# The low parts of sixteen input tiles and eight gate tiles: their subtraction moves from VectorE to GpSimd

## The chip, the cores and the metric

The kernel runs on one core of a Trainium2 chip. The metric is the device time of one execution in microseconds (us). Engines are named as in the profile: PE is TensorE, DVE is VectorE, ACT is ScalarE, POOL is GpSimd and SP is SyncE. PEld is TensorE's loading of weights, which overlaps its matmuls. Each engine works through its own queue in order, and an instruction that waits for a semaphore holds up all that stands behind it in that queue.

## The reference, cut to what matters

One inference step of two layers over 640 tokens (512 latent, 128 context), width 1024, in fp32. Layer 0 is attention and a feed-forward, layer 1 a gated linear recurrent unit and a feed-forward.

```python
def _swiglu(x, w_gu, w_down):
    gate, up = jnp.split(x @ w_gu, 2, axis=-1)
    return (jax.nn.silu(gate) * up) @ w_down

def _rglru_coeffs(xc, w_a, b_a, w_i, b_i, lam):
    ...
    r = jax.nn.sigmoid(jnp.einsum('btnk,nkj->btnj', xb, w_a).reshape(B, T, D) + b_a)
    i = jax.nn.sigmoid(jnp.einsum('btnk,nkj->btnj', xb, w_i).reshape(B, T, D) + b_i)
    ...

def _lru_mixer(xm, h0, w_in, conv_w, conv_b, w_a, b_a, w_i, b_i, lam, w_out):
    gate, xr = jnp.split(xm @ w_in, 2, axis=-1)
    ...
    return y @ w_out, jnp.stack([hT_f, hT_b], axis=1)
```

The tiles of the change belong to `w_in` (1024 x 2048, the recurrent unit's input weights) and to `w_a` and `w_i` (its gate weights). They are prepared in the first feed-forward and used in the recurrent unit after it.

## The kernel before

**Products in three terms.** TensorE multiplies in fp32r, a shorter form of fp32. To keep precision, every operand is split into a high part (its value cast to fp32r) and a low part (value minus high part, again fp32r). A product is three matmuls in one PSUM bank: high by high (line 245), high by low input (246), low weight by high input (247). Weights are tiles of 128 x (8 x 128), so 128 x 1024; inputs are held transposed, with 640 token columns, which go in two chunks of 320. One weight tile (a "unit") thus has 2 x 8 x 3 = 48 matmuls.

**Splitting a weight.** `unit` loads the raw tile on SyncE's queue, casts it on ScalarE (line 189, `whi` or `whx`), and subtracts on VectorE (line 194, `wlo` or `wlx`). For most weights this is done just ahead of their use. The recurrent unit's input weights (`in_wi`, 16 tiles of 128 x 1024) and gate weights (`in_wg`, 8 tiles of 128 x 512) have their low parts made earlier, during the first feed-forward, and written to DRAM. There SyncE's queue reads them back when the recurrent unit runs: line 191 for `lowi`, line 1433 for `lowg`.

**The first feed-forward** (`ffn`, layer 0) has three groups of 8, 7 and 7 hidden tiles of 128. For each hidden tile, a gate unit and an up unit run. VectorE scales the gate's PSUM (line 1042), ScalarE applies SiLU (1044), VectorE scales the up's PSUM (1050) and multiplies (1053), and the product is split (ScalarE's cast at 1551, VectorE's low part at 1553, tiles `big`). After each group, `project` multiplies by the down weights and VectorE adds each result to the residual `x` (line 673). PSUM banks for chunks are three called `mm` and two called `mx`; a bank is free for a new chunk when VectorE has read it.

**The early low parts** (`lows`, a generator). `request` loads a tile twice on GpSimd's queue: cast to fp32r into `mprod` (one buffer, line 307), and plain into `mraw` (two buffers, line 309). The subtraction of line 316 then writes the low part over `mraw`, and line 319, on GpSimd's queue, stores it to DRAM. Then the next tile is requested. `ahead` hands out these steps: each call adds 2 to an account, a large tile costs 3 and a small one 2; it is called once for every gate or up unit after hidden tile 12, and for every tile of the down-projections of the second and third group. `pin` keeps an instruction behind a named one in the order of the program. That order is otherwise set by a scheduler, which simulates a timeline.

The same two tags, `mprod` and `mraw`, serve the modulation columns before (`mod_cols`: GpSimd's queue loads `mraw` at line 270, VectorE multiplies and sums at line 274). Behind the last low part, GpSimd's next work is line 633, a small step of the norm ahead of the recurrent unit.

Of the kernel before, what the change touches and what calls it, by code (L numbers as in the profile page):

```python
# [9 lines left out]
F32 = mybir.dt.float32  # L10
F32R = mybir.dt.float32r
AF = mybir.ActivationFunctionType
ALU = mybir.AluOpType
# [116 lines left out]
class _Step:  # L130
# [170 lines left out]
    def lows(self):  # L301
        nc = self.nc

        def request(key, src):
            shape = list(src.shape)
            hi = self.t(shape, F32R, "mprod", 1, self.sb)
            nc.gpsimd.dma_start(hi, src)
            raw = self.t(shape, F32R, "mraw", 2, self.sb)
            nc.gpsimd.dma_start(raw.bitcast(F32), src)
            return key, raw, hi  # L310
        held = request(*self.split_ahead[0])
        yield 3
        for n in range(len(self.split_ahead)):
            key, raw, hi = held
            with self.pin(self.done):
                nc.vector.tensor_tensor(raw, raw.bitcast(F32), hi.bitcast(F32), ALU.subtract)  # L316
            shape = list(raw.shape)
            self.low_parts[key] = self.dram.tile(shape, F32, tag=f"low{key[0]}{key[1]}", name=f"low{key[0]}{key[1]}")
            nc.gpsimd.dma_start(self.low_parts[key], raw.bitcast(F32))
            if n + 1 < len(self.split_ahead):  # L320
                held = request(*self.split_ahead[n + 1])
            yield 3 if shape[1] == KT else 2
# [794 lines left out]
    def project_halves(self, w, hi, lo, gk, key, xd, ended, opening):  # L1117
# [23 lines left out]
        both = sides[0] + sides[1]  # L1141
        highs(KT - 3, both)
        lows(KT - 3, both)
        highs(KT - 2, both)
        for f in (3, 4):
# [18 lines left out]
        with self.pin(self.done):  # L1164
            lows(KT - 2, both)
        lows(KT - 1, sides[0])
        added = self.added
        part(3, ((0, hi), (0, lo)))
# [562 lines left out]
```

## Time and profile before

| what | value |
| --- | --- |
| median of 3 runs | 1506.03 us (1503.84 to 1506.76) |
| the profiled execution | 1504.18 us, of which its span is 1502.4 us |
| TensorE busy | 1471.8 us, 98% of the span |
| VectorE busy | 1067.6 us, 71% |
| ScalarE busy | 700.0 us, 47% |
| GpSimd busy | 270.3 us, 18% |
| line 316, 24 times | first start 569.2 us, last 751.9 us |

The span runs from the first to the last instruction of the profiled execution, and times in rows count from its start. A row of a group reads: line, engine, operation, output <- inputs by the program's names, shapes, count | busy us, mean ns of one | idle us of that engine just ahead of the group, and what ended most of it. A row of the timeline reads: start, duration, engine, line, operation, names, shape, and in brackets the engine's idle time ahead of it with its releaser. "issue" as a releaser means that the profile shows nothing that the engine waited for. The granted TensorE clock was 0.999 of full speed over the span.

### The profile page before, as it was taken

The numbers are of one execution on the slowest core, as the hardware profiler recorded it, in microseconds if no ns is written. First come the engines' busy times: TensorE is split into PE (matmuls) and PEld (weight loads), VectorE is DVE, ScalarE is ACT, GpSimd is POOL, SyncE is SP. The second block draws the span as 40 slices with busy tenths as digits, with TensorE's granted clock in tenths as the row PEclk, the third lists the DMA queues.
The fourth block names the chain that finished last, engine by engine and source line by source line (L and its number), as shares of the span: only waits on it lengthen the run. The fifth ranks groups of instructions, "written<-read, shape, count | busy, mean of one in ns | idle before, by whom it ended". The sixth has DMA issues, their size and how long they took to land. (4 is left out here: it accounts for less than half of the span.)

```text
span 1502.4 us, 26467 instructions
## 1 busy us (share of the span) xinstructions
PE 1471.8 (98%) x10463; PEld 1442.7 (96%) x10463; DVE 1067.6 (71%) x2035; ACT 700.0 (47%) x1277; POOL 270.3 (18%) x344
## 2 busy tenths in 40 slices
PE   9999999999999999999999999999999999999997
PEld 7999999899999999989899999999999999999997
DVE  5778998689999997544454669786975665655655
ACT  5676666664332123211232479874634342524243
POOL 0212232101111111212200110000331323232311
PEclk9999999999999999999999999999999999999999
DMA  9645765345666667776631454445243131313221
GB/s 377 200 127 180 194 185 168 99 165 181 196 187 195 209 200 259 263 265 222 203 94 51 131 186 139 138 132 214 96 139 98 57 113 57 113 57 101 69 57 70
DMA packets 83547, 232.45 MB, mean 155 GB/s; under 512 B 9408, under 2 KB 25952, under 8 KB 83296
## 3 DMA queue, kind: packets, MB, share of 16 engines
q1 hardware_dynamic: 57360, 142.31, 29.3%
q0 software_dynamic: 25456, 87.77, 18.5%
q8 instruction: 82, 1.34, 0.4%
q10 hardware_dynamic: 608, 0.69, 0.1%
q14 instruction: 41, 0.34, 0.1%
HBM read 204.12 MB, written 19.41 MB: 149 GB/s over the span
## 5 line engine op out<-in xcount | busy, mean ns | idle before, releaser
L245 PE MATMUL mm<-big,whi 128*128 128x320 f32 (+3 forms) x1193 | 368.1, 310 | 4.2 <-ACT gl L1565 1.5
L246 PE MATMUL mm<-big,whi 128*128 128x320 f32 (+3 forms) x1193 | 370.8, 311 | 0.6 <-DVE big L1553 0.6
L247 PE MATMUL mm<-big,wlo 128*128 128x320 f32 (+3 forms) x1193 | 368.7, 310 | 0.0
L245 PEld LDWEIGHTS mm<-big,whi 128*128 128x128 f32 x1193 | 223.9, 188 | 6.8 <-ACT gl L1565 2.1
L246 PEld LDWEIGHTS mm<-big,whi 128*128 128x128 f32 x1193 | 224.3, 188 | 2.2 <-DVE big L1553 1.1
L247 PEld LDWEIGHTS mm<-big,wlo 128*128 128x128 f32 x1193 | 224.6, 188 | 1.1
L274 DVE SCALAR_TENSOR_TENSOR mprod<-mraw,csb 128x1024 f32<-128x1024 f32 x160 | 195.2, 1220 | 10.2 <-DMA mraw<-in_wm 9.5
L673 DVE SCALAR_TENSOR_TENSOR x<-mm,G,x 128x128 f32<-128x128 f32 (+3 forms) x193 | 77.8, 434 | 63.0 <-PE mm L247 61.6
L245 PE MATMUL mm<-big,whx 128*128 128x320 f32 (+3 forms) x363 | 112.3, 309 | 4.8 <-DVE up L1050 1.9
L189 ACT CAST whi<-raw 128x1024 fp32r<-128x1024 f32 (+1 forms) x70 | 72.8, 1040 | 92.3 <-PE mm L246 61.0
L246 PE MATMUL mm<-big,whx 128*128 128x320 f32 (+3 forms) x363 | 112.4, 310 | 1.9 <-DVE big L1553 1.9
L247 PE MATMUL mm<-big,wlx 128*128 128x320 f32 (+3 forms) x363 | 112.2, 309 | 0.0
L270 POOL DMA_DIRECT2D mraw<-in_wm x80 | 43.4, 543 | 345.1 <-DVE mprod L274 258.8
L194 DVE TENSOR_TENSOR wlo<-raw,whi 128x1024 fp32r<-128x1024 f32 (+1 forms) x71 | 85.6, 1206 | 12.6 <-ACT whi L189 12.5
L245 PE MATMUL mx<-big,whi 128*128 128x320 f32 (+3 forms) x299 | 92.1, 308 | 0.7 <-DVE sg L1042 0.7
L246 PE MATMUL mx<-big,whi 128*128 128x320 f32 (+3 forms) x299 | 92.1, 308 | 0.0
L247 PE MATMUL mx<-big,wlo 128*128 128x320 f32 (+3 forms) x299 | 91.8, 307 | 0.0
L316 DVE TENSOR_TENSOR mraw<-mraw,mprod 128x1024 fp32r<-128x1024 f32 (+1 forms) x24 | 25.1, 1048 | 80.4 <-DMA mprod<-in_wi 43.0
L189 ACT CAST whx<-raw 128x1024 fp32r<-128x1024 f32 (+1 forms) x38 | 38.9, 1023 | 81.8 <-PE mm L246 48.5
L245 PE MATMUL mx<-big,whx 128*128 128x320 f32 (+3 forms) x234 | 72.5, 310 | 2.1 <-DVE up L1050 2.1
L245 PEld LDWEIGHTS mm<-big,whx 128*128 128x128 f32 x363 | 68.4, 188 | 5.6 <-DVE up L1050 2.2
L1551 ACT CAST whi<-raw 128x1024 fp32r<-128x1024 f32 (+1 forms) x41 | 41.3, 1007 | 68.3 <-PE mm L246 43.6
(421 smaller groups left out, 3878.4 us busy)
## 6 DMA issues: line engine op xcount, KB each, us to landing
raw<-in_gu SPq DMA_DIRECT2D x88, 512.0 KB, 3.7
mraw<-in_wm POOLq DMA_DIRECT2D x80, 512.0 KB, 3.9
raw<-in_dn SPq DMA_DIRECT2D x24, 512.0 KB, 3.6
sw<-in_wm SPq DMA_DIRECT2D x16, 512.0 KB, 10.2
raw<-in_wqk SPq DMA_DIRECT2D x16, 512.0 KB, 5.0
mraw<-in_wi POOLq DMA_DIRECT2D x16, 512.0 KB, 5.0
mprod<-in_wi POOLq DMA_DIRECT2D x16, 512.0 KB, 5.9
lowi<-mraw POOLq DMA_DIRECT2D x16, 512.0 KB, 2.9
```

The lines of the kernel that those rows point to most:

```text
L189: nc.scalar.copy(hi, raw)
L194: self.low = nc.vector.tensor_tensor(lo, raw, hi.bitcast(F32), ALU.subtract).ins
L245: nc.tensor.matmul(ps, hi[:, k], xhi[:, k, s], start=(k == 0), stop=False)
L246: nc.tensor.matmul(ps, hi[:, k], xlo[:, k, s], start=False, stop=False)
L247: self.done = nc.tensor.matmul(ps, lo[:, k], xhi[:, k, s], start=False, stop=(k == last)).ins
L270: nc.gpsimd.dma_start(w, self.i["wm"][l * 6 + j - 2, f])
L274: nc.vector.scalar_tensor_tensor(prod, w, 1.0, self.csb[:, s], ALU.mult, ALU.mult, accum_out=out[:, s, f:f + 1])
L316: nc.vector.tensor_tensor(raw, raw.bitcast(F32), hi.bitcast(F32), ALU.subtract)
L673: self.added = self.nc.vector.scalar_tensor_tensor(xs, ps[:, a - t0:b - t0], G[:, s, f:f + 1], xs, ALU.mult, ALU.add).ins
L1551: self.nc.scalar.copy(hi, v)
```

## The change

In `lows`, the subtraction is issued on GpSimd instead of VectorE; its operands, its pin, and the loads and the store around it are as they were.

```diff
         for n in range(len(self.split_ahead)):
             key, raw, hi = held
             with self.pin(self.done):
-                nc.vector.tensor_tensor(raw, raw.bitcast(F32), hi.bitcast(F32), ALU.subtract)
+                nc.gpsimd.tensor_tensor(raw, raw.bitcast(F32), hi.bitcast(F32), ALU.subtract)
             shape = list(raw.shape)
             self.low_parts[key] = self.dram.tile(shape, F32, tag=f"low{key[0]}{key[1]}", name=f"low{key[0]}{key[1]}")
             nc.gpsimd.dma_start(self.low_parts[key], raw.bitcast(F32))
```

The scheduler's order changes with it on three engines; ScalarE's and SyncE's queues read the same as before.

VectorE, from the end of the second down-projection (`x` is the residual, fed by PSUM banks `mm` and `mx`) into the third group's gate and up units (`sg`, `up`). `mraw` and `mprod` are the tile to be split and its high part:

```order
 L673 SCALAR_TENSOR_TENSOR x_4130<-mx_7992,G_680_3223,x_4130 128x320
-L316 TENSOR_TENSOR mraw_8760<-mraw_8760,mprod_8758 128x1024
 L673 SCALAR_TENSOR_TENSOR x_4130<-mm_8015,G_680_3223,x_4130 128x192
 L673 SCALAR_TENSOR_TENSOR x_4130<-mm_8015,G_680_3223,x_4130 128x128
 L194 TENSOR_TENSOR wlo_8409<-raw_8406,whi_8408 128x1024
 L1042 TENSOR_TENSOR sg_8081<-mm_8054,r_4705 128x320
-L316 TENSOR_TENSOR mraw_8831<-mraw_8831,mprod_8829 128x512
 L1042 TENSOR_TENSOR sg_8081<-mx_8085,r_4705 128x320
 L194 TENSOR_TENSOR wlx_8478<-raw_8475,whx_8477 128x1024
-L316 TENSOR_TENSOR mraw_8971<-mraw_8971,mprod_8969 128x512
 L1050 TENSOR_TENSOR up_8152<-mm_8125,r_4705 128x320
```

Three subtractions leave this part of VectorE's queue, and what stands around them keeps its order.

GpSimd's queue at the same place:

```order
 L309 DMA mraw_8831<-in_wg 128x512
+L316 TENSOR_TENSOR mraw_8760<-mraw_8760,mprod_8758 128x1024
 L319 DMA lowi_8827<-mraw_8760 128x1024
 L307 DMA mprod_8829<-in_wg 128x512
 L309 DMA mraw_8971<-in_wg 128x512
+L316 TENSOR_TENSOR mraw_8831<-mraw_8831,mprod_8829 128x512
 L319 DMA lowg_8967<-mraw_8831 128x512
 L307 DMA mprod_8969<-in_wg 128x512
```

Each subtraction stands just ahead of the store of its own result, behind the plain load of the next tile; the DMA issues keep their order.

TensorE, at the start of the second down-projection, where two `mm` banks are filled from the last hidden tile's high part (`big_6420`) and low part (`big_6421`):

```order
 L245 MATMUL mm_7609<-big_6420,whx_7582 128x320
 L246 MATMUL mm_7609<-big_6421,whx_7582 128x320
+L246 MATMUL mm_7586<-big_6421,whx_7582 128x320
+L247 MATMUL mm_7586<-big_6420,wlx_7583 128x320
 L247 MATMUL mm_7609<-big_6420,wlx_7583 128x320
 L245 MATMUL mx_7646<-big_6420,whi_7642 128x320
```

The two matmuls that close bank `mm_7586` stood nine rows further down before. Nothing else moves on TensorE.

## The prediction

> **What bounds the kernel now.** I read the page's totals first, then busy time by stretch, the lines of TensorE inside the stretch, the line that is moved, and the timelines of VectorE, TensorE and GpSimd around one stall.
>
> ```profile
> span 1502.4 us, 26467 instructions
> PE 1471.8 (98%) x10463; PEld 1442.7 (96%) x10463; DVE 1067.6 (71%) x2035; ACT 700.0 (47%) x1277; POOL 270.3 (18%) x344
> ```
>
> TensorE is the bound: 98% of the span. A change that takes work from VectorE is worth only what TensorE now waits for it. The stretch is found by busy time (columns: length; TensorE, its weight loads, VectorE, ScalarE, GpSimd; granted clock; DMA).
>
> ```profile
> 569.00:590.00 21.00, 21.00 (x145) 21.00 (x144) 16.32 (x28) 6.12 (x12) 3.76 (x7) 1.00 0.64 229
> 590.00:755.00 165.00, 153.51 (x1033) 151.49 (x1032) 80.05 (x129) 34.96 (x66) 35.52 (x66) 1.00 0.71 240
> 755.00:820.00 65.00, 65.00 (x431) 65.00 (x430) 32.93 (x60) 21.29 (x44) 0.00 (x0) 1.00 0.25 73
> ```
>
> The 24 moved subtractions run from 569 to 752 us. In the first row TensorE never stops; in the second it lacks 165.00 - 153.51 = 11.5 us; in the third, the same feed-forward without the subtractions, it lacks nothing. All 11.5 us end on VectorE, or on ScalarE behind it (idle time and releaser stand last, for 560 to 770 us):
>
> ```profile
> L246 PE MATMUL mm<-big,whx 128*128 128x320 f32 (+1 forms) x137 | 42.6, 311 | 1.9 <-DVE big L1553 1.9
> L245 PE MATMUL mm<-big,whx 128*128 128x320 f32 (+1 forms) x137 | 42.6, 311 | 4.8 <-DVE up L1050 1.9 <-ACT big L1551 1.7 <-DVE x L673 1.2
> L245 PE MATMUL mm<-big,whi 128*128 128x320 f32 (+1 forms) x131 | 40.6, 310 | 1.9 <-DVE up L1050 1.5 <-DVE x L673 0.4
> L245 PE MATMUL mx<-big,whi 128*128 128x320 f32 (+1 forms) x92 | 28.5, 310 | 0.7 <-DVE sg L1042 0.7
> L245 PE MATMUL mx<-big,whx 128*128 128x320 f32 (+1 forms) x85 | 26.3, 310 | 2.1 <-DVE up L1050 2.1
> ```
>
> VectorE is busy for only 80 of these 165 us, so it is not short of time. It stands still in front of the line that is moved:
>
> ```profile
> L316 DVE TENSOR_TENSOR mraw<-mraw,mprod 128x1024 fp32r<-128x1024 f32 (+1 forms) x24 | 25.1, 1048 | 80.4 <-DMA mprod<-in_wi 43.0 <-DMA mprod<-in_wg 24.0 <-issue 13.4
> ```
>
> 25.1 us of work and 80.4 us of standing, mostly for the load of the high part: 105.5 us in which nothing behind it in VectorE's queue can run. How that reaches TensorE (VectorE first, then TensorE's idle times):
>
> ```profile
> 692.85 1.22 DVE L316 TENSOR_TENSOR mraw<-mraw,mprod 128x1024 fp32r<-128x1024 f32 x1 [4.86 <-DMA mprod<-in_wi]
> 694.00 0.67 DVE L673 SCALAR_TENSOR_TENSOR x<-mm,G,x 128x192 f32<-128x192 f32 x2
> 694.58 1.22 DVE L194 TENSOR_TENSOR wlx<-raw,whx 128x1024 fp32r<-128x1024 f32 x1
> 695.71 0.55 DVE L673 SCALAR_TENSOR_TENSOR x<-mx,G,x 128x320 f32<-128x320 f32 x1
> 701.38 1.23 DVE L316 TENSOR_TENSOR mraw<-mraw,mprod 128x1024 fp32r<-128x1024 f32 x1 [5.12 <-DMA mprod<-in_wi]
> 710.23 0.69 DVE L316 TENSOR_TENSOR mraw<-mraw,mprod 128x512 fp32r<-128x512 f32 x1 [5.50 <-DMA mprod<-in_wg]
> ```
>
> ```profile
> 694.81 0.39 PE L245 MATMUL mm<-big,whi 128*128 128x322 f32 x1 [0.41 <-DVE x L673]
> 703.34 0.39 PE L245 MATMUL mm<-big,whx 128*128 128x322 f32 x1 [1.22 <-DVE x L673]
> 711.38 0.41 PE L245 MATMUL mx<-big,whi 128*128 128x322 f32 x1 [0.73 <-DVE sg L1042]
> ```
>
> Between two subtractions VectorE finds about 2.5 us of work (0.67, 1.22, 0.55), then waits 5 us for the next load. It empties PSUM at the pace of that load, one turn in 8.5 us, and TensorE stalls for a free bank about a microsecond after each of these three subtractions starts. The eight stalls of the stretch all follow one of the 24 in this way.
>
> **The change part by part.** Removed from VectorE: 24 subtractions and the waits before them, 105.5 us. What that frees on the path is the 11.5 us. If nothing takes their place, the profiled 1504.18 us (a span of 1502.4 and 1.8 around it, 1.85 below the median of the runs) become 1492.7.
>
> Added to GpSimd: the same 24. No row shows GpSimd writing fp32r, so the price is bounded by its two-input operations on fp32 (shortest, median, longest ns):
>
> ```profile
> L1219 POOL TENSOR_TENSOR sum<-raw,raw x19: 1289/1302/2013, 1084.1 to 1434.1; 128x512 f32<-128x512 f32 x19
> L1107 POOL TENSOR_TENSOR x<-x,c x4: 1001/1490/3651, 1077.9 to 1091.4; 128x320 f32<-128x320 f32 x4
> ```
>
> Line 1219 has one of the two sizes, 128x512: 1.3 us, and by doubling 2.6 us for 128x1024. Line 1107 scaled from 320 to 1024 columns gives 4.8 us by its median and 11.7 by its longest. I take 2.6 and 1.3, from the row of the same width.
>
> The loop on GpSimd's queue: subtract, store (L319), load the next high part (L307), wait for it, subtract.
>
> ```profile
> 694.37 0.54 POOL L319 DMA_DIRECT2D lowi<-mraw  x1 [4.56 <-DVE mraw L316]
> 694.90 0.54 POOL L307 DMA_DIRECT2D mprod<-in_wi  x1
> 589.49 1.23 DVE L316 TENSOR_TENSOR mraw<-mraw,mprod 128x1024 fp32r<-128x1024 f32 x1 [2.39 <-DMA mprod<-in_wi]
> 751.94 0.69 DVE L316 TENSOR_TENSOR mraw<-mraw,mprod 128x512 fp32r<-128x512 f32 x1 [3.56 <-DMA mprod<-in_wg]
> ```
>
> From the subtraction's start (692.85) to its store is 1.52 us; it becomes 2.6, so a turn lengthens by 1.1. The 15 turns from 589.49 to 710.23 took 8.05 us each and would take 9.13; the seven from 710.23 to 751.94 took 5.96 each and, 0.3 longer, would take 6.26. The last subtraction starts near 589.5 + 137 + 44 = 770 and ends at 772. Behind it on GpSimd's queue stands the norm's line 633, which nobody wants before:
>
> ```profile
> 835.39 0.87 POOL L633 TENSOR_TENSOR rs<-var,mhalf 128x3 f32<-128x3 f32 x1 [81.91 <-DVE var L631]
> 836.48 0.32 SPq L191 DMA_DIRECT2D wlo<-lowi  x1
> ```
>
> With TensorE 11.5 us earlier that is 824, so 52 us are left, and the first read of a low part (SyncE, second row) comes after it. GpSimd's longer loop is covered. That cover is gone when a 128x1024 subtraction takes over 2.6 + 52/19 = 5.3 us (15 large ones and eight halves count as 19).
>
> VectorE's first wait after the change is for the modulation weights, which GpSimd now requests 1.1 us later, behind the longer first subtraction:
>
> ```profile
> 577.38 1.23 DVE L274 SCALAR_TENSOR_TENSOR mprod<-mraw,csb 128x1024 f32<-128x1024 f32 x1 [1.88 <-DMA mraw<-in_wm]
> ```
>
> Cost 0 to 1.1 us; I take 0, since TensorE stood nowhere in that stretch and VectorE has a 1.23 us subtraction and a wait less ahead of it.
>
> Two matmuls move: at the start of the second down-projection, the last two of one chunk now stand nine matmuls earlier, 9 x 153.51/1033 = 1.3 us. They need the low part of the last hidden tile:
>
> ```profile
> 644.77 0.42 PE L246 MATMUL mm<-big,whx 128*128 128x320 f32 x1 [1.91 <-DVE big L1553]
> 643.09 1.23 DVE L316 TENSOR_TENSOR mraw<-mraw,mprod 128x1024 fp32r<-128x1024 f32 x1 [2.23 <-issue]
> ```
>
> The subtraction ahead of that tile held it for 2.23 + 1.23 = 3.46 us. Gone, this pays the 1.91 of the stall and the 1.3, barely. Cost 0 to 1.3; I take 0.2.
>
> Contention. When GpSimd and VectorE both work on SBUF tiles, they take turns (GpSimd, VectorE beside it, the same VectorE operation undisturbed):
>
> ```profile
> 1084.13 1.55 POOL L1219 TENSOR_TENSOR sum<-raw,raw 128x512 f32<-128x512 f32 x1
> 1082.93 1.58 DVE L1553 TENSOR_TENSOR big<-x,big 128x320 fp32r<-128x320 f32 x1
> 1095.02 0.48 DVE L1553 TENSOR_TENSOR big<-g,big 128x320 fp32r<-128x320 f32 x1
> ```
>
> 1.58 us instead of 0.48: VectorE lost 1.1 us to one GpSimd operation of 1.3 us. At worst each of the 24 holds VectorE for its whole length: 16 x 2.6 + 8 x 1.3 = 52 us, half of the 105.5 that go. In proportion TensorE would stall 11.5 x 52/105.5 = 5.7 us; at best 0. What decides is a later stretch in which GpSimd adds beside a VectorE busier than it will be here:
>
> ```profile
> 1100.00:1440.00 340.00, 339.75 (x2316) 338.89 (x2315) 202.62 (x327) 129.09 (x208) 99.99 (x72) 1.00 0.28 86
> ```
>
> 100 us of GpSimd additions, and TensorE lacks 0.25 of 340 us. I take 0.3, and keep 5.7 for the range. [...]
>
> Sum: 11.5 - 0 - 0.2 - 0.3 = 11.0 us. The profiled execution would be 1493.2, the median 1506.03 - 11.0 = 1495.0.
>
> **The rivals.** *Lock.* Every subtraction blocks VectorE for its length, as in the 1.58 us row: 1506.0 - 11.5 + 5.7 = 1500.2. Against it stands the row of 340 us.
>
> *No gain.* Another wait lies right behind each stall (a cast on ScalarE, a weight load), and the 11.5 us return under other names: 1504 to 1506. Against it: 65.00 of 65.00 us busy at 755 to 820, and 21.00 of 21.00 at the start, with the same code around.
>
> *Slower.* GpSimd is slow at fp32r, or loses turns to VectorE, as line 1107 did at its longest. Past 5.3 us per subtraction line 633 runs late and TensorE stands at the closing norm; past 2.6 + (52 + 11.5)/19 = 5.9 us the gain is eaten. At 8.25, midway between 4.8 and 11.7, the loop ends 107 us later, at 879, 55 late: 1506.0 - 11.5 + 55 = 1549.5. For it speaks only the longest of line 1107's four.
>
> **How the numbers follow.** Forecast 0.75, lock 0.11, no gain 0.08, slower 0.06. A measurement of this kernel can tell about 0.2%, 3 us. Forecast and lock are both faster: 0.86; unchanged 0.08; slower 0.06. The range starts at the whole 11.5 us off a median that may lie 2.2 lower (the fastest run, 1503.84): 1492.3. It ends just above the lock's 1500.2, at 1501; outside lie no gain and slower, 0.14. The forecast alone spans 1492.3 to 1498.
>
> **What would show it.** VectorE's idle time before line 316 is gone, and TensorE is busy for over 164 of any 165 us in this stretch. GpSimd shows 16 operations of about 2.6 us and 8 of 1.3, the last ending near 772, and line 633 still waits tens of microseconds for VectorE. Wrong: TensorE idle behind VectorE operations stretched by a microsecond or more (lock), TensorE idle behind other releasers (no gain), line 633 starting right after line 319 (slower).

## The result, and the profile after

The changed kernel takes 1491.15 us (median of 4 runs, 1490.91 to 1492.21); beside it the kernel before takes 1506.39 (4 runs, 1503.84 to 1507.95). The ratio is 0.9902, with a 95% interval of 0.9885 to 0.9919. The forecast of 1495.0 had the direction, the place and the mechanism right and the size too small: the time lies 1.15 us below the range's low end of 1492.3. The profiled execution took 1491.32 us, against 1493.2 forecast for it.

The page's totals after:

```profile
span 1489.6 us, 26442 instructions
PE 1470.3 (99%) x10463; PEld 1443.2 (97%) x10463; DVE 1063.6 (71%) x2011; ACT 702.7 (47%) x1277; POOL 321.8 (22%) x368
```

The 24 instructions went from VectorE (2035 to 2011) to GpSimd (344 to 368), and 12.8 us went from the span. VectorE is hardly less busy (1067.6 to 1063.6 us), though 25.1 us of work left it; its timeline below shows why. Busy time by stretch, with the columns as in the prediction; the last row is for a later comparison:

```profile
569.00:590.00 21.00, 21.00 (x145) 21.00 (x144) 14.80 (x27) 5.93 (x13) 5.97 (x8) 1.00 0.59 201
590.00:755.00 165.00, 165.00 (x1124) 165.00 (x1124) 83.90 (x126) 45.10 (x82) 78.34 (x82) 1.00 0.75 246
755.00:820.00 65.00, 65.00 (x425) 65.00 (x425) 28.65 (x48) 15.83 (x32) 6.85 (x9) 1.00 0.27 86
821.80:860.00 38.20, 37.93 (x281) 37.60 (x280) 26.61 (x71) 20.76 (x45) 6.52 (x16) 1.00 0.61 192
```

TensorE lacked 11.5 of 165 us here before; now it lacks nothing, and it starts 1124 matmuls where it started 1033. These 91 matmuls, at the 165.00/1124 = 0.147 us of the same row, are some 13.4 us: more than the idle time that is gone. The prediction's error is already in this one row.

GpSimd, all of line 316 (shortest, median, longest ns, first and last start):

```profile
L316 POOL TENSOR_TENSOR mraw<-mraw,mprod x24: 1284/2394/3052, 570.4 to 768.4; 128x1024 fp32r<-128x1024 f32 x16, 128x512 fp32r<-128x512 f32 x8
```

GpSimd's timeline, one subtraction in the middle and the last one with what follows:

```profile
691.11 2.39 POOL L316 TENSOR_TENSOR mraw<-mraw,mprod 128x1024 fp32r<-128x1024 f32 x1 [2.91 <-DMA mprod<-in_wi]
...
768.36 1.29 POOL L316 TENSOR_TENSOR mraw<-mraw,mprod 128x512 fp32r<-128x512 f32 x1 [3.46 <-DMA mprod<-in_wg]
769.97 0.58 POOL L319 DMA_DIRECT2D lowg<-mraw  x1 [0.31 <-POOL mraw L316]
822.05 0.88 POOL L633 TENSOR_TENSOR rs<-var,mhalf 128x3 f32<-128x3 f32 x1 [51.51 <-DVE var L631]
```

GpSimd now does the standing (2.91 us for the load of the high part, 3.46 at the end), and nobody wants anything of its queue: line 633 waits 51.51 us for VectorE.

VectorE's timeline in the second down-projection, then beside the subtraction at 691.11:

```profile
677.39 0.68 DVE L673 SCALAR_TENSOR_TENSOR x<-mm,G,x 128x192 f32<-128x192 f32 x2 [2.52 <-PE mm L247]
678.33 1.23 DVE L194 TENSOR_TENSOR wlx<-raw,whx 128x1024 fp32r<-128x1024 f32 x1 [0.26 <-ACT whx L189]
680.47 0.55 DVE L673 SCALAR_TENSOR_TENSOR x<-mx,G,x 128x320 f32<-128x320 f32 x1 [0.91 <-PE mx L247]
691.56 3.02 DVE L194 TENSOR_TENSOR wlx<-raw,whx 128x1024 fp32r<-128x1024 f32 x1 [0.45 <-ACT whx L189]
694.51 0.48 DVE L1050 TENSOR_TENSOR up<-mm,r 128x320 f32<-128x320 f32 x1
```

The releasers have turned round: line 673 waited behind line 316's load before, and now waits for TensorE (2.52 and 0.91 us). The fourth row is what the prediction's rival *Lock* is about: a line 194 that takes 1.23 us alone takes 3.02 beside GpSimd's subtraction. It costs VectorE time, and TensorE none in this stretch (165.00 of 165.00 us busy).

### The profile page after: what moved, and what is told of

Read it like the earlier page. It is cut to its first block, busy times and chain, and to the rows that moved or that the text cites. A ratio compares the mean times of both kernels' runs of the same rounds, so it can differ in the third digit from the quotient of the medians.

```text
span 1489.6 us, 26442 instructions
## 1 busy us (share of the span) xinstructions
PE 1470.3 (99%) x10463; PEld 1443.2 (97%) x10463; DVE 1063.6 (71%) x2011; ACT 702.7 (47%) x1277; POOL 321.8 (22%) x368
## 5 line engine op out<-in xcount | busy, mean ns | idle before, releaser
L194 DVE TENSOR_TENSOR wlo<-raw,whi 128x1024 fp32r<-128x1024 f32 (+1 forms) x71 | 87.8, 1237 | 13.6 <-ACT whi L189 13.6
L1219 POOL TENSOR_TENSOR sum<-raw 128x512 f32<-128x512 f32 x19 | 25.6, 1349 | 223.8 <-DMA raw<-in_gu 146.5
L247 PE MATMUL mx<-big,wlx 128*128 128x320 f32 (+3 forms) x234 | 72.6, 310 | 0.0
```

What stands on the lines that cost most here:

```text
L194: self.low = nc.vector.tensor_tensor(lo, raw, hi.bitcast(F32), ALU.subtract).ins
L247: self.done = nc.tensor.matmul(ps, lo[:, k], xhi[:, k, s], start=False, stop=(k == last)).ins
```

## The experiments

Each theory had the same facts to explain: 25.1 us of work and 80.4 us of standing left VectorE, and TensorE gained some 13 us. The standing theory says that only the wait in VectorE's queue mattered. Its rivals: the 25 us of work mattered; GpSimd's new work still costs something; the cover of 52 us is thinner than it looks.

**Work without the wait.** On the kernel before, VectorE subtracts two resident tiles of the same size, and so waits for no load (the pin moves too, from the last matmul to the last subtraction of line 194):

```diff
-            with self.pin(self.done):
-                nc.vector.tensor_tensor(raw, raw.bitcast(F32), hi.bitcast(F32), ALU.subtract)
+            with self.pin(self.low):
+                m = KT * P if key[0] == "i" else 4 * P; nc.vector.tensor_tensor(self.t([P, KT * P], F32R, "mhigh", 1, self.sb)[:, 0:m], self.csb[:, 0, 0:m], self.csb[:, 1, 0:m], ALU.subtract)
```

> VectorE keeps 24 subtractions of the old sizes at about the old places, but takes them from tiles that lie ready (the conditioning vectors), into a scratch tile; nothing waits for a load there. The loads and stores of the early tiles go on without a subtraction (what is stored are the raw tiles). Theory 'standing': only the wait in front of the subtraction cost anything, the 25 us of work nothing: 1490.5 to 1493 us, TensorE idle under 1 us between 569 us and the norm's line 633. Rival 'work': the work itself held TensorE up, at least in its share of the 105.5 us, 25/105.5 of about 14 us, so 3 us or more: 1494.5 to 1500 us.

Measured: 1491.53 us (1490.99 to 1491.86, 4 runs), ratio 0.9924 (0.9907 to 0.9942). VectorE's group, and the stretch:

```profile
L316 DVE TENSOR_TENSOR mhigh<-csb 128x1024 fp32r<-128x1024 f32 (+1 forms) x24 | 25.0, 1040 | 0.0
```

```profile
590.00:744.00 154.00, 154.00 (x1050) 154.00 (x1049) 83.97 (x134) 41.56 (x75) 35.27 (x65) 1.00 0.80 264
```

All 25.0 us of work are back on VectorE with no idle time ahead of them, and TensorE stands nowhere. The work was worth nothing. It does not lie at quite the old places: the 24 start between 576.4 and 790.4 us, where they had started between 569.2 and 751.9.

**The wait without the work.** On the changed kernel, VectorE first subtracts one column of both loaded tiles into a scratch column, so it waits for the same loads:

```diff
+                col = lambda t: t.rearrange(...)[:, 0:1].bitcast(F32); nc.vector.tensor_tensor(self.t([P, 1], F32, "mhigh", 1, self.sb), col(raw), col(hi), ALU.subtract)
                 nc.gpsimd.tensor_tensor(raw, raw.bitcast(F32), hi.bitcast(F32), ALU.subtract)
```

> The changed kernel, and VectorE in addition reads one column of both loads of each early tile (128x1, 24 times) before GpSimd subtracts. VectorE thus stands for the same loads with next to no work. Theory 'standing': the stalls come back, 1500 to 1507 us, with VectorE idle 60 us or more in front of these 24. Rival 'work': 1491 to 1493 us, as the changed kernel.

Measured: 1500.99 us (1498.30 to 1506.71, 10 runs), ratio 0.9989 (0.9973 to 1.0004). VectorE's group, TensorE's longest stall in the second group's down-projection, and the granted clock around it (the last but two of a row's numbers):

```profile
L316 DVE TENSOR_TENSOR mhigh<-mraw,mprod 128x1 f32<-128x1 f32 x24 | 3.8, 159 | 82.8 <-DMA mprod<-in_wi 54.3 <-DMA mprod<-in_wg 24.1 <-issue 4.4
```

```profile
643.29 0.63 PE L245 MATMUL mm<-big,whx 128*128 128x320 f32 x1 [3.93 <-ACT big L1551]
```

```profile
638.00:643.00 5.00, 1.35 (x10) 1.09 (x8) 3.33 (x5) 0.22 (x1) 2.83 (x2) 0.92 0.43 145
...
647.00:649.00 2.00, 2.00 (x9) 2.00 (x8) 1.22 (x2) 0.00 (x0) 0.00 (x0) 0.50 1.07 383
649.00:651.00 2.00, 2.00 (x15) 2.00 (x15) 0.45 (x2) 0.00 (x0) 1.08 (x1) 1.00 0.98 344
```

3.8 us of work and 82.8 of standing bring nearly the whole time back. The pair of runs settles it: with the work and without the wait the gain is whole; with the wait and almost no work, nothing that can be told from no change is left of it. The last view shows something that no row of before had: behind this stall of 3.93 us TensorE runs at a granted clock of 0.50, 9 matmuls in 2 us instead of 15. More on this below.

**No subtraction at all.** On the changed kernel, the line is left out:

```diff
-                nc.gpsimd.tensor_tensor(raw, raw.bitcast(F32), hi.bitcast(F32), ALU.subtract)
+                pass
```

> The changed kernel without the 24 subtractions on any engine; loads and stores stay (what is stored are the raw tiles). Theory 'free on GpSimd': the same as the changed kernel within 0.5 us, 1490.7 to 1492 us. Rival 'lock': VectorE and TensorE still pay for turns taken with GpSimd, so this one is 1 to 5.7 us faster, 1485.5 to 1490 us.

Measured: 1490.94 us (1490.38 to 1492.38, 4 runs), ratio 0.9921 (0.9906 to 0.9937), so 0.2 us from the changed kernel's median, within both spreads. VectorE's line groups from 569 to 800 us, first of the changed kernel, then of this one:

```profile
L194 DVE TENSOR_TENSOR wlx<-raw,whx 128x1024 fp32r<-128x1024 f32 (+1 forms) x17 | 23.7, 1392 | 4.9 <-ACT whx L189 4.9
L1053 DVE SCALAR_TENSOR_TENSOR sg<-up,bias,sg 128x192 f32<-128x192 f32 (+2 forms) x36 | 18.8, 551 | 0.8
```

```profile
L194 DVE TENSOR_TENSOR wlx<-raw,whx 128x1024 fp32r<-128x1024 f32 (+1 forms) x17 | 19.8, 1162 | 5.0 <-ACT whx L189 4.9
L1053 DVE SCALAR_TENSOR_TENSOR sg<-up,bias,sg 128x192 f32<-128x192 f32 (+2 forms) x36 | 14.8, 438 | 0.8
```

VectorE's loss beside GpSimd's subtractions is real, 230 ns on average on each of these line 194s and 113 ns on each line 1053, and these runs show no price of it for the kernel. It is also where most of VectorE's busy time stayed: 3.9 and 4.0 us here, and 13.94 us from 569 to 821 us (VectorE is busy for 127.81 us there in the changed kernel and for 113.87 here).

**Three subtractions for one.** To see where GpSimd's work would begin to cost, it is done three times:

```diff
-                nc.gpsimd.tensor_tensor(raw, raw.bitcast(F32), hi.bitcast(F32), ALU.subtract)
+                for out in (raw, hi, hi): nc.gpsimd.tensor_tensor(out, raw.bitcast(F32), hi.bitcast(F32), ALU.subtract)
```

> The changed kernel with each subtraction on GpSimd done three times (the second and third into the spent high part), so about 7.2 us for a large tile and 3.9 for a small one. Theory 'cover of 52 us': the loop on GpSimd's queue ends 19 x 4.8 = 91 us later, near 860, and the norm's line 633, wanted at 822, runs near 861: 39 us late, 1530 us (1515 to 1545). Rival: the queue's end decides nothing, 1491 to 1494 us.

Measured: 1505.93 us (1503.48 to 1507.85, 8 runs), ratio 1.0027 (1.0010 to 1.0043). Some 0.3% slower than the kernel before, but far from the 1530 expected. GpSimd's timeline at the norm:

```profile
830.79 1.30 POOL L316 TENSOR_TENSOR mprod<-mraw,mprod 128x512 fp32r<-128x512 f32 x1
832.04 0.88 POOL L633 TENSOR_TENSOR rs<-var,mhalf 128x3 f32<-128x3 f32 x1
...
849.56 1.27 POOL L316 TENSOR_TENSOR mraw<-mraw,mprod 128x512 fp32r<-128x512 f32 x1
```

Line 633 started right behind a subtraction, as the rival *Slower* said it would, but at 832.04 and not behind the last one: the scheduler's new order put it ahead of the last tiles. The miss is an order that I had taken as fixed. The other part of the loss is contention (VectorE's group, TensorE's stall, and TensorE's busy time at the norm):

```profile
L1053 DVE SCALAR_TENSOR_TENSOR sg<-up,bias,sg 128x192 f32<-128x192 f32 (+2 forms) x36 | 38.2, 1087 | 0.8
```

```profile
642.53 0.41 PE L246 MATMUL mm<-big,whx 128*128 128x320 f32 x1 [3.16 <-DVE big L1553]
```

```profile
826.00:850.00 24.00, 19.20 (x149) 18.34 (x148) 17.45 (x35) 6.67 (x13) 14.69 (x17) 1.00 0.73 238
```

Line 1053 takes 1087 ns instead of 438, and the last hidden tile's low part comes late enough to stall TensorE for 3.16 us. At the norm TensorE lacks 4.8 of 24 us, where the changed kernel lacks 0.27 of 38.20. So VectorE's loss does cost here, where GpSimd subtracts most of the time: it is busy for 110.82 of the 154 us from 590 to 744, and for 88.88 with the two subtractions of the next run, which lose nothing. Cover and contention were not separated by a run of their own. The profile splits them in part: by the measure of the next section, 5.7 us of the 12.2 that this execution lost against the changed kernel (1503.48 against 1491.32) are gone before line 633 is wanted, and so are no matter of the cover; the rest is lost from there on, where both act.

**Two subtractions for one.** The same with `(raw, hi)`, to test the cover of 52 us inside its bounds.

> The changed kernel with each subtraction on GpSimd done twice (the second into the spent high part): 4.8 us for a large tile, 2.6 for a small one, under the 5.3 us at which the prediction let the cover of line 633 end. Theory 'covered': the last one ends near 770 + 19 x 2.4 = 815 us, the norm's line 633 still waits for VectorE, TensorE idles under 1 us: 1491 to 1493 us. Rival 'turns': three times the operation gave a stall of 3.2 us at the start of the second down-projection, where the last hidden tile waits for VectorE; twice gives one of 1 to 2 us there, and up to two windows of half clock if it is longer than about 2.3: 1493.5 to 1498 us.

Measured: 1491.15 us (1490.84 to 1492.41, 5 runs), ratio 0.9928 (0.9903 to 0.9953). GpSimd's timeline at the norm, and the stretch:

```profile
811.97 1.29 POOL L316 TENSOR_TENSOR mprod<-mraw,mprod 128x512 fp32r<-128x512 f32 x1
...
821.41 0.88 POOL L633 TENSOR_TENSOR rs<-var,mhalf 128x3 f32<-128x3 f32 x1 [7.62 <-DVE var L631]
```

```profile
590.00:744.00 154.00, 154.00 (x1049) 154.00 (x1048) 90.06 (x114) 40.59 (x74) 88.88 (x66) 1.00 0.65 218
```

The loop ends 44 us later than in the changed kernel (811.97 against 768.36), line 633 still waits 7.62 us for VectorE, and nothing is lost. The cover is as large as predicted. The rival's 2.3 us and its half clock are those of two runs below: a stall of 2.31 us (input tiles back) was followed by a granted clock of 0.50 for 3.42 us, one of 2.80 (second buffer) for 6.82.

**Only the input tiles back on VectorE, and only the gate tiles.** On the changed kernel, in two runs:

```diff
+                (nc.vector if key[0] == "i" else nc.gpsimd).tensor_tensor(raw, raw.bitcast(F32), hi.bitcast(F32), ALU.subtract)
```

> The changed kernel with the sixteen large subtractions (input weights) back on VectorE, the eight small ones on GpSimd. Theory 'standing': the stalls that followed the large ones before (1.66, 1.91, 0.41 and 1.22 us, each with 0.26) come back, 6.2 us: 1497.4 us, 1493 to 1502. Rival 'only the small ones matter': 1491 to 1492.5 us.

```diff
+                (nc.vector if key[0] == "g" else nc.gpsimd).tensor_tensor(raw, raw.bitcast(F32), hi.bitcast(F32), ALU.subtract)
```

> The changed kernel with the eight small subtractions (gate weights) back on VectorE, the sixteen large ones on GpSimd. Theory 'standing, and a stall costs more than its idle time': the stalls that followed the eight small ones before (0.73, 1.50, 1.95 and 2.11 us, each with some 0.26 us for the broken chain of matmuls) come back, 7.3 us: 1498.5 us, 1494 to 1503 since the waits hang on when loads land. Rival 'only the large ones matter': 1491 to 1492.5 us.

Input tiles back: 1497.67 us (1494.12 to 1500.31, 7 runs), ratio 0.9955 (0.9938 to 0.9973), for 1497.4 expected. That it is so close is partly luck: in place of the four stalls expected (1.66, 1.91, 0.41 and 1.22 us) the profile has three, of 2.31, 0.67 and 0.83, and a granted clock of 0.50 for 3.42 us behind the first. Gate tiles back: 1500.23 us (1494.22 to 1502.66, 10 runs), ratio 0.9959 (0.9941 to 0.9976), inside the 1494 to 1503 expected, but not in the way expected. TensorE's worst stall and its clock, with the input tiles back:

```profile
641.12 0.63 PE L245 MATMUL mm<-big,whx 128*128 128x320 f32 x1 [2.31 <-ACT big L1551]
```

```profile
590.00:700.00 110.00, 106.98 (x716) 106.23 (x715) 54.21 (x84) 22.18 (x39) 22.45 (x42) 0.98 0.80 273
```

With the gate tiles back, VectorE's first small subtraction, TensorE's one stall behind it, and the clock after it:

```profile
730.39 0.69 DVE L316 TENSOR_TENSOR mraw<-mraw,mprod 128x512 fp32r<-128x512 f32 x1 [20.78 <-DMA mprod<-in_wg]
```

```profile
733.14 0.64 PE L245 MATMUL mm<-big,whx 128*128 128x322 f32 x1 [6.60 <-DVE up L1050]
```

```profile
733.00:737.00 4.00, 3.86 (x14) 3.86 (x15) 3.58 (x7) 1.38 (x6) 1.44 (x3) 0.50 0.71 200
```

I had expected the four short stalls that the gate tiles caused before. What came is one of 6.60 us: in this order VectorE reached the first small subtraction long before its load, and stood for 20.78 us with TensorE's banks behind it. Each part alone costs, and the two losses do not add up to the whole: what decided here is where a load lands against VectorE's queue, not the number of subtractions.

**A second buffer for the high part.** On the kernel before, VectorE keeps the subtraction, and every other tile loads its high part into another buffer, so that the load can be issued one tile earlier:

```diff
-            hi = self.t(shape, F32R, "mprod", 1, self.sb)
+            hi = self.t(shape, F32R, "mhigh" if len(self.low_parts) % 2 else "mprod", 1, self.sb)
```

> The kernel before, with VectorE subtracting, but a second buffer for the high parts: odd tiles load theirs into a tile of their own, so that this load needn't wait for the subtraction ahead. Theory 'standing': VectorE stands under half of the 80 us in front of line 316 and most of the gain comes without GpSimd, 1491 to 1497 us. Rival: the plain load, which must wait for the store of the tile two back, comes late next, and VectorE stands as long as before: 1499 to 1507 us.

Measured: 1494.52 us (1492.78 to 1496.85, 4 runs), ratio 0.9932 (0.9907 to 0.9958). VectorE's two groups of line 316, and TensorE's one stall:

```profile
L316 DVE TENSOR_TENSOR mraw<-mraw,mhigh 128x1024 fp32r<-128x1024 f32 (+1 forms) x12 | 12.6, 1047 | 53.2 <-DMA mraw<-in_wi 38.6 <-DMA mraw<-in_wg 14.6
L316 DVE TENSOR_TENSOR mraw<-mraw,mprod 128x1024 fp32r<-128x1024 f32 (+1 forms) x12 | 12.5, 1043 | 10.0 <-DMA mraw<-in_wi 5.3 <-DMA mprod<-in_wi 3.2 <-DMA mraw<-in_wg 1.3
```

```profile
641.48 0.64 PE L245 MATMUL mm<-big,whx 128*128 128x320 f32 x1 [2.80 <-ACT big L1551]
```

Most of the gain without GpSimd, as expected; but VectorE still stands for 53.2 + 10.0 = 63.2 us, where under 40 was expected, now for the plain load `mraw`. Only one stall reaches TensorE. So the sum of VectorE's standing is not a measure of the loss either: 80.4 us of it cost 13.6 us, and 63.2 cost 5.7, each in its profiled execution (by the account in the next section).

**The kernel before, profiled once more**, to see what one stall costs beyond its recorded idle time.

> The kernel before, unchanged, for a second profile of it. Theory 'each stall costs its idle time, some 0.26 us for the broken chain, and after a stall of more than about 3 us a stretch at half clock': the norm's line 631, at 821.8 us in the changed kernel, comes at 821.8 plus TensorE's idle time in the stretch plus 0.26 per stall plus half of any time at half clock, within 0.5 us. Rival 'TensorE is a little slower all through the stretch': 821.8 plus the idle time plus 2 us, whatever the number of stalls.

Measured: 1505.99 us, a span of 1504.2. TensorE's worst stall, the clock after it, and VectorE's first step of the norm:

```profile
641.75 0.41 PE L245 MATMUL mm<-big,whx 128*128 128x320 f32 x1 [2.39 <-ACT big L1551]
```

```profile
642.00:643.00 1.00, 1.00 (x6) 1.00 (x6) 0.20 (x1) 0.00 (x0) 0.18 (x1) 0.58 0.95 352
644.00:645.00 1.00, 1.00 (x5) 1.00 (x5) 0.75 (x1) 0.00 (x0) 0.00 (x0) 0.50 0.89 299
645.00:646.00 1.00, 0.82 (x4) 0.45 (x3) 1.00 (x3) 0.00 (x0) 0.23 (x1) 0.71 1.03 393
```

```profile
836.60 0.16 DVE L631 TENSOR_SCALAR var<-at 128x3 f32<-128x3 f32 x1 [0.60 <-PE at L629]
```

A clock of 0.58, then 0.50, then 0.71 in these microseconds is half clock from 642.16 to 645.58, or 3.42 us. It came behind a stall of 2.39 us. The 3 us from which I had expected it was an estimate of mine: in the earlier runs it had followed stalls of 3.93 and 2.92 us (wait only) and 3.16 (three subtractions), and none of the stalls of before, up to 2.11 us. TensorE inside it:

```profile
642.38 0.47 PE L246 MATMUL mm<-big,whx 128*128 128x320 f32 x1
...
645.04 0.47 PE L247 MATMUL mx<-big,wlo 128*128 128x320 f32 x1
```

From the first row to the second are ten steps of the chain in 2.66 us, so a matmul starts every 0.27 us instead of every 0.147: 45% of the time is lost, 1.5 us of the 3.42. Line 631 at 836.60 is what the next section is about: stalls that cost only their idle time and this half clock would put it near 821.80 + 10.55 + 1.5 = 833.9, and 0.26 us more for each of the nine near 836.2, inside the theory's 0.5 us. The rival's 2 us for the whole stretch would put it near 835.9; with nine stalls the two are too close to tell apart. The kernels with three stalls and with one do tell them apart, in the next section.

## Why the prediction was wrong in size, and right in kind

**The failed step is the first term of the sum, 11.5 us.** I took TensorE's recorded idle time for all that TensorE loses. How much it lost can be measured from a matmul ahead of the stretch to the norm's line 631, which needs everything before it. TensorE's first gate matmul, of before and of after:

```profile
563.16 0.30 PE L245 MATMUL mm<-big,whx 128*128 128x322 f32 x1
```

```profile
563.44 0.30 PE L245 MATMUL mm<-big,whx 128*128 128x322 f32 x1
```

And line 631 of before and of after, on VectorE:

```profile
835.08 0.16 DVE L631 TENSOR_SCALAR var<-at 128x3 f32<-128x3 f32 x1 [0.60 <-PE at L629]
```

```profile
821.80 0.16 DVE L631 TENSOR_SCALAR var<-at 128x3 f32<-128x3 f32 x1 [0.60 <-PE at L629]
```

835.08 - 563.16 = 271.92 us before, 821.80 - 563.44 = 258.36 after: 13.56 us, not 11.5. Eight stalls share the missing 2.1 us. TensorE's timeline around the one that the prediction quotes at 644.77 shows how (before):

```profile
642.55 0.31 PE L245 MATMUL mx<-big,whi 128*128 128x320 f32 x1
...
645.02 0.31 PE L247 MATMUL mm<-big,wlx 128*128 128x320 f32 x1
645.17 0.31 PE L246 MATMUL mx<-big,whi 128*128 128x320 f32 x1
```

In a running chain a matmul starts every 0.15 us and lasts 0.31, so each overlaps the next. Idle time counts only from the end of the last one: from 642.55 to 644.77 it is 2.22 us from start to start, of which 1.91 is written as idle. The matmul behind the stall takes 0.42 and the next starts 0.25 later. So this stall costs (2.22 - 0.15) + (0.25 - 0.15) = 2.17 us, 0.26 more than its record.

The account of every profiled execution, worked out in the same way (us; "lost" is line 631's time minus the anchor's, minus 258.36; half clock is 45% of the time at a granted clock of 0.50 in which TensorE was not idle):

| kernel | lost | recorded idle | stalls | half clock | left per stall |
| --- | --- | --- | --- | --- | --- |
| before | 13.56 | 11.49 | 8 | 0 | 0.26 |
| before, once more | 14.46 | 10.55 | 9 | 1.53 | 0.26 |
| input tiles back | 6.23 | 3.81 | 3 | 1.36 | 0.35 |
| wait only | 14.03 | 7.42 | 3 | 5.36 | 0.42 |
| gate tiles back | 9.0 | 6.60 | 1 | 2.17 | 0.23 |
| second buffer | 5.74 | 2.80 | 1 | 2.75 | 0.19 |
| three subtractions | 5.72 | 3.43 | 2 | 1.53 | 0.38 |
| work only, no subtraction, two subtractions | within 0.04 | 0 | 0 | 0 | |

An example of the fifth column: in the wait only, 13.65 us ran at half clock, 1.73 of them inside stalls, where half clock takes nothing more; 11.92 x 0.45 = 5.36. Recorded idle time, 0.26 us a stall and half clock together give each of the seven losses within 0.5 us. The rival of the last run falls here: were TensorE slower by some 2 us all through the stretch, whatever the number of stalls, the two kernels with one stall would have 2 us left over, and they have 0.2. The profiled executions of wait only, gate tiles back and second buffer are the slowest of their runs (1506.71, 1502.66 and 1496.85 us), so their rows show more than these kernels lose as a rule.

**Point by point.**

- *Removed, 11.5 us*: measured 13.56, as above. The span gained 12.8 of it: the anchor is 0.28 later in the profiled execution after, and another 0.5 goes between line 631 and the end. I did not trace these.
- *Modulation load, 0 of 0 to 1.1*, and *two moved matmuls, 0.2 of 0 to 1.3*: TensorE is busy 21.00 of 21.00 and 165.00 of 165.00 us. Both cost nothing.
- *Contention, 0.3 of 0 to 5.7*: 0. VectorE gave back some of its time, TensorE none, as the run without a subtraction shows. The line 194 that takes 3.02 us waits out GpSimd's subtraction in the trace, to 0.15 us: the subtraction ends at 691.11 + 2.39 = 693.50, 1.23 more is 694.73, and line 194 ends at 694.58. (The prediction's own pair of rows was mismatched: its GpSimd row starts at 1084.13, after VectorE's at 1082.93; what held VectorE there was the addition before, from 1082.62 for 1.54 us.) What decided, as I read it, is that VectorE, no longer standing, had 81 of 165 us to spare; with three subtractions, where it was busy for 105.10 of 154 us, TensorE did lose. The rival *Lock* priced that loss in the proportion that standing had cost; as I read it, a delay of 1 to 2 us after which VectorE catches up is not the same as a turn of 8.5 us.
- *GpSimd's price, 2.6 and 1.3 us*: medians 2.39 and 1.29. The last subtraction ended at 769.65 (772 forecast), and the cover of 52 us was 51.51, which the doubled subtraction used up to 7.62 without loss. The end at 769.65 is so close partly by luck: the second subtraction started at 592.84 and not 589.49, and the fifteen turns from there took 8.76 us each and not 9.13.
- *The rival "no gain"*: no other wait took the place of the stalls.
- *The base and the range*: the low end took off 11.5 us from the fastest of three runs. Over all comparisons the kernel before ran 46 times, with a median of 1503.26 us (1496.78 to 1509.28), so the three runs shown lay 2.8 us above its middle. Of the 3.85 us between 1495.0 and 1491.15, 2.8 are this and 1.1 is the sum itself (12.1 us of gain against that median, for 11.0). In the profiled executions, which don't depend on the base, the sum is 12.8 for 11.0: 2.1 of the stalls and 0.5 of costs that did not come, less the 0.8 that is not traced. A range that let the 11.5 us grow by what a broken chain costs would have held the time.

## What to carry to other kernels

In this kernel a subtraction that waited for its load held up what stood behind it on VectorE: 80.4 us of standing cost TensorE 13.56. Put such an instruction on an engine whose queue nobody needs soon, even if the work takes twice as long there (2.39 us against 1.23 here), and count how long that queue can run late before it is wanted (51.51 us here). When you price a stall of TensorE, don't stop at its recorded idle time (11.49 of the 13.56 us here): compare when a later step starts, or count the matmuls of the stretch at their undisturbed pace.

## What the runs showed of the hardware that was not expected

**Half clock came behind a stall of 2.31 us, and not behind one of 3.47.** Stalls recorded as up to 2.11 us (the longest of the profile of before) left the granted clock at 1.00. In the runs above, those of 2.31 (input tiles back), 2.39 (before, once more) and 3.16 us (three subtractions) were followed by 0.50 for about 3.41 us, those of 2.80 (second buffer), 3.93 and 2.92 (wait only) and 6.60 (gate tiles back) by 0.50 for about 6.8. Each 3.41 us of it cost up to 1.5, at the 45% above. But the longest stall of the three subtractions, at the norm, left the clock as it was; the row from 826 to 850 us above has it inside, at a clock of 1.00:

```profile
846.35 0.49 PE L626 MATMUL at<-ones,ssq 128*128 128x128 f32 x2 [3.47 <-DVE ssq L612]
```

The granted clock, read from the traces in stretches of 0.5 us, shows in what the two kinds differ. Within each of these executions the times at which it changed lie whole multiples of 3.413 us apart (wait only: 642.19, 649.02, 768.48 and 775.31, so 2, 35 and 2 steps). Continue this grid through the six executions with half clock, from 560 to 835 us (to 850 with three subtractions): every step at full clock with 1.94 us or more of idle time was followed by half clock, and none with 1.89 or less. The profiled executions of before and after, from 10 us up to TensorE's last matmul, have no step with more than 1.65 us, and no half clock. Of the stall of 2.31 us, 1.94 lie in one step; the one of 3.47 is cut at 844.76 into 1.89 and 1.59. A step at half clock with 0.63 us or more of idle time was followed by another one, a step with 0.38 or less was not: so the stall of 2.80 gave two (0.71 of it reached into the first), and that of 3.16 gave one. These limits are read off the traces that they describe, and the 3.413 us from the times in them; no run was made to test them.

**Standing spreads the times.** Four kernels in which VectorE waits for no load here (the changed one, work only, no subtraction, two subtractions) lie within 0.9 to 2.0 us each, and the fifth, three subtractions, within 4.4; the wait only spreads over 8.4 us, gate tiles back over 8.4, input tiles back over 6.2, and the kernel before over 12.5. Half clock behind some stalls and not others is part of it: of gate tiles back, six runs had a granted clock of 0.996 and took 1500.10 to 1502.66 us, and four had 0.998 or 0.999 and took 1494.22 to 1496.69. It is not all of it: the kernel before took 1496.78 to 1507.81 us in runs with a clock of 0.999, which leaves room for a loss of some 2 us by half clock. What makes the rest is not shown.
